# A two-layer streaming encoder in float32: the first chunk's norm from token-major x, the u columns of the next group turned one product earlier, and B's weight pieces moved off the v steps

## The chip, the cores and the metric

The kernel runs on one core of a Trainium2 chip. The metric is the device time of one execution in microseconds (us), the median of several runs. Five engines work side by side, each through its own list of instructions in a fixed order: PE (TensorE, matrix products), DVE (VectorE), ACT (ScalarE), POOL (GpSimd) and SP (SyncE, which here only issues DMA transfers). An engine stops at an instruction whose inputs are not there, and everything behind it on that engine stops too.

## The reference

The stream `x` has 2048 tokens of 1024 channels. Layer A mixes by causal pooling, layer B by stick-breaking attention; after each comes a gated embedding add.

```python
def pool_mixer(h, w_in, w_group, scale, w_out):
    u, z = jnp.split(h @ w_in, 2, axis=-1)
    ...   # means over the last 2, 4, 8, 16 frames in four channel groups, minus the frame itself
    mixed = jnp.einsum('bsgc,gcd->bsgd', pooled, w_group).reshape(B, S, D_MODEL) * scale
    return (mixed * jax.nn.silu(z)) @ w_out
...
h = rms_norm(x, a_norm[i])
x = x + pool_mixer(h, a_w_in[i], a_w_group[i], a_scale[i], a_w_out[i])
kv_in = rms_norm(x, kv_norm)
k_all, v_all = jnp.split(kv_in @ w_kv, 2, axis=-1)
k_sh = rms_norm(split_heads(k_all), k_norm)
q, z = jnp.split(rms_norm(x, b_norm[j]) @ b_w_in[j], 2, axis=-1)
q = rms_norm(split_heads(q), b_q_norm[j])
o = stick_breaking_attention(q, k_sh, v_sh)
x = x + (o * jax.nn.silu(z)) @ b_w_out[j]
x = x + (p[i] @ ple_w[i]) * jax.nn.sigmoid(x @ ple_gate_w[i])
```

## The kernel before

**Numbers in two halves.** Every float32 operand is split into a rounded high half and the remainder. ACT writes the high half, DVE or POOL the low one, and PE makes three products of each pair (high by high, high by low, low by high; lines 164 to 166). A pair of a weight is a *unit*, tile `wpair`, from two pools of six; its raw form is `wraw`.

**Chunks and steps.** The dense part runs over four chunks of 512 tokens. A chunk has 22 steps (`STEPS`): z and u columns of the four groups in turn (steps 0 to 7: z3, u3, z2, u2, z1, u1, z0, u0), the output projection (8 to 11), the gate (12 to 15), then two steps each for q, k and v (16 to 21). Ahead of a step the loop at line 806 converts the next step's weights and fetches those of the step after it. The attention follows the fourth chunk.

**Folding in the first chunk.** The linear map of a group is folded into the u columns, once, in chunk 0. `load_fold` (line 396) asks for the columns (`uraw`, two tiles of 128x1024) and for the group's map. `fold` (line 410) works in eight pieces: four times `across` (line 417) turns a part of the columns into a pair `wt`, four times `mapped` (line 424) makes 12 matmuls (line 431) and converts the result into a unit (lines 438 and 439), which the group's u step multiplies by and which is stored to DRAM for the later chunks. Group 3 is folded inside step z3 (`first_beside`); group g-1 inside the u step of group g (`second_beside`, line 455): columns in the first four of the product's eight parts, `mapped` behind parts 5 to 8.

**The norm of the first chunk.** The squares of all eight `x` tiles (channels by tokens) are taken on ACT (line 326) and summed on DVE (328); `summed` (299) turns the sum with four small matmuls, POOL makes the inverse root, and `bcast` (240) lays it over the partitions. z3 and u3 are scaled by it (485, 503), then come the running sums (509), the gate and the halves `mp` of the result.

**Order.** The engines' lists are made by a scheduler that may move instructions; `tc.keep_in_program_order` pins one to its place in the program. SP issues its transfers in program order (`queue`, line 87). The pinned ones here are those of step z3 and of group 3's fold.

**B's pieces.** 56 pieces of layer B's weights (`kept`) are fetched, split and stored beside the dense steps; line 835 decides at which.

Of the kernel before, what the change touches and what calls it, by code (L numbers as in the profile page):

```python
# [14 lines left out]
P = 128  # L15
# [19 lines left out]
def trunk_kernel(ctx, tc, x, xt, pt0, wut, cols, heads, zin, grp, aout, agate, aple,  # L35
# [63 lines left out]
    class Weights:  # L99
# [29 lines left out]
        def convert(self, half=0):  # L129
            kk, n, gain, kept, c0 = self.kk, self.n, self.gain, self.kept, self.c0  # L130
            self.reread()
            for k0 in self.part(half):
# [6 lines left out]
                if gain is None:  # L139
                    self.stay(A.copy(out=pr[:, 0], in_=raw))  # L140
                    state["w"] += 1
                    (G if state["w"] % 3 else V).tensor_tensor(out=pr[:, 1], in0=raw, in1=f(pr[:, 0]), op=ALU.subtract)  # L142
# [74 lines left out]
    with ExitStack() as st:  # L217
# [59 lines left out]
        def load_tokens(s, q):  # L277

            xn = f(pair("xn")).rearrange("q e n -> q (e n)")
            t0 = s * W5 + q * P  # L280
            queue(out=xn, in_=x[0, t0 : t0 + P, :])
            chunk[s].setdefault("xn", []).append(xn)

        def prep(s):
# [14 lines left out]
            def summed():  # L299
                acc = chunk[0].pop("acc0")  # L300
                ps = turned()
                for j in range(4):
                    T.matmul(ps[:, 0, j : j + 1], acc[:, j * P : (j + 1) * P], ones, start=True, stop=True)
                A.copy(out=parts, in_=ps[:, 0, 0:4])
                norm()

            if not s:
                chunk[0]["summed"] = summed
# [13 lines left out]
            if s:  # L322
                return
            for o in range(KT):
                sq = tmp("sqx")
                stay(A.activation(out=sq, in_=xs[o], func=AF.Square))
                if o:
                    V.tensor_tensor(out=acc, in0=acc, in1=sq, op=ALU.add)
                else:
                    acc = sq  # L330
                if o % 4 == 3:
                    yield
            chunk[0]["acc0"] = acc

        wz0 = {"raw": [], "pair": []}

        def load_first(g):
# [3 lines left out]
            for q in range(4):  # L341
# [4 lines left out]
                if not q:  # L346
                    load_gains()
# [24 lines left out]
        def first_beside():  # L372
# [6 lines left out]
            def behind():  # L379
                for kt in range(KT):  # L380
                    next(lead, None)
                    if kt == 7:
                        for _ in lead:
                            pass
                        chunk[0]["fold"][2] = load_fold(2)
# [3 lines left out]
                    if kt > 2:  # L389
                        next(folded, None)  # L390
                    yield
# [4 lines left out]
        def load_fold(g):  # L396
# [3 lines left out]
            if g < 3:  # L400
                maps[g] = Weights(grp[g], 2, 0, 256)
                maps[g].fetch()
            for ct in range(2):
# [3 lines left out]
                raws.append(raw)  # L407
            return raws, wg

        def fold(g, raws, wg):  # L410
# [4 lines left out]
            stay = tc.keep_in_program_order if g == 3 else lambda ins: ins  # L415
# [29 lines left out]
            for i in range(4):  # L445
                across(i)
                if i == 2 and g < 3:
                    maps[g].convert()
# [5 lines left out]

        def second_beside(g):
# [764 lines left out]
```

## Time and profile before

| | us |
|---|---|
| median of three runs | 2733.45 |
| lowest, highest | 2730.84, 2734.16 |
| the profiled execution, its own time | 2732.34 |
| its span, first to last instruction | 2730.6 |

The page gives busy times of 2688.7 us for PE, 1983.8 for DVE, 1366.5 for ACT and 879.0 for POOL. Times in the trace count from the first instruction. In a row of the timeline stand start, length, engine, line, operation, tiles and, in brackets, the idle time just before it with what ended it. Matmuls are pipelined, so the distance of two starts, and not the length shown, is what one costs.

### The profile page before, as it was taken

How to read it: one execution, taken by the hardware profiler on the slowest of the kernel's cores; microseconds unless marked ns; L12 is line 12 of the kernel's file. 1: busy time of each engine (PE TensorE's matmuls, PEld its weight loads, DVE VectorE, ACT ScalarE, POOL GpSimd, SP SyncE). 2: the span in 40 equal slices, each digit the busy share in tenths (PEclk: the TensorE clock that was granted, in tenths of full speed). 3: DMA queues.
4: the chain of work that ended last, by engine and by line, in shares of the span. 5: the costliest groups of instructions: out<-in, count | busy, mean ns of one | idle time of the engine just before them, and what ended most of it. 6: DMA issues, size and time to landing. Idle time of an engine off the chain costs nothing.

```text
span 2730.6 us, 38583 instructions
## 1 busy us (share of the span) xinstructions
PE 2688.7 (98%) x13360; PEld 2228.9 (82%) x13360; DVE 1983.8 (73%) x2572; ACT 1366.5 (50%) x2672; POOL 879.0 (32%) x695
## 2 busy tenths in 40 slices
PE   8999999999999999999999999999999999999999
PEld 7888888888888888888878888887887778888877
DVE  6777635665366643755399999999999998997632
ACT  5445532455234541445356556666666665655430
POOL 2574337643485435753121111110110111112220
PEclk9999999999999999999999999999999999999999
DMA  7646696466955679444688675555555566668965
GB/s 276 219 158 234 247 321 218 167 238 247 319 190 192 231 259 317 143 148 158 215 249 276 190 226 169 167 163 170 173 156 166 162 198 208 192 200 258 268 227 170
DMA packets 275968, 579.46 MB, mean 212 GB/s; under 512 B 33047, under 2 KB 66839, under 8 KB 275773
## 3 DMA queue, kind: packets, MB, share of 16 engines
q1 hardware_dynamic: 270034, 569.31, 63.5%
q10 hardware_dynamic: 5738, 7.68, 1.0%
q8 instruction: 106, 1.74, 0.3%
q14 instruction: 90, 0.73, 0.1%
HBM read 436.30 MB, written 132.19 MB: 208 GB/s over the span
## 4 chain that ended last, share of the span: by engine, by line
PE 81%; DVE 10%; issue 3%; DMA 2%; POOL 2%; ACT 1%; SPq 1%; ACTq 0%; DVEq 0%; POOLq 0%
PE psd L613 18%; PE psd L164 8%; PE psd L165 8%; PE psd L166 8%; PE psa L939 7%; PE psd L983 5%; PE psd L985 5%; PE psd L987 5%; DVE pp L926 4%; PE pso L952 3%; PE psl L915 3%; PE pso L951 3%; PE psl L914 3%; DVE at L943 2%; PE pst L718 1%
## 5 line engine op out<-in xcount | busy, mean ns | idle before, releaser
L942 ACT CAST at<-psa 128x512 fp32r<-128x512 f32 (+3 forms) x640 | 334.8, 523 | 481.6 <-PE psa L939 463.8
L613 PE MATMUL psd<-wpair,x 128*128 128x512 f32 x2304 | 537.5, 392 | 0.9 <-DVE x L254 0.9
L926 DVE TENSOR_TENSOR_SCAN pp<-kap,pp,zeros 128x512 f32<-128x512 f32 x384 | 514.7, 1340 | 3.0 <-ACT kap L918 2.5
L613 PEld LDWEIGHTS psd<-wpair,x 128*128 128x128 f32 x2304 | 429.8, 188 | 88.9 <-DVE x L254 1.7
L943 DVE TENSOR_TENSOR at<-psa,at 128x512 fp32r<-128x512 f32 (+3 forms) x640 | 381.1, 596 | 82.9 <-ACT at L942 79.5
L939 PE MATMUL psa<-ident,pp 128*128 128x128 f32 x2176 | 346.9, 275 | 21.5 <-DVE at L943 20.2
L918 ACT ACTIVATE kap<-psl 128x512 f32<-128x512 f32 (+3 forms) x640 | 345.2, 539 | 14.0 <-PE psl L915 11.2
L939 PEld LDWEIGHTS psa<-ident,pp 128*128 128x128 f32 x2176 | 262.9, 140 | 98.1 <-DVE at L943 45.8
L914 PE MATMUL psl<-kk,qa 128*128 128x512 f32 (+3 forms) x640 | 281.9, 440 | 0.0
L952 PE MATMUL pso<-at,vv 128*128 128x512 f32 (+3 forms) x640 | 234.7, 367 | 0.8 <-DVE at L943 0.8
L915 PE MATMUL psl<-kk,qb 128*128 128x512 f32 (+3 forms) x640 | 232.7, 364 | 0.0
L951 PE MATMUL pso<-at,vv 128*128 128x512 f32 (+3 forms) x640 | 231.9, 362 | 0.0
L923 DVE TENSOR_TENSOR_SCAN pp<-kap,ahead 128x128 f32<-128x128 f32 (+3 forms) x256 | 223.9, 875 | 5.3 <-ACT kap L918 3.9
L164 PE MATMUL psd<-xp,wpair 128*128 128x512 f32 x512 | 201.6, 394 | 3.6 <-DVE wpair L439 3.5
L165 PE MATMUL psd<-xp,wpair 128*128 128x512 f32 x512 | 200.6, 392 | 2.1 <-DVE xp L314 2.1
L166 PE MATMUL psd<-xp,wpair 128*128 128x512 f32 x512 | 200.4, 392 | 0.0
L147 DVE SCALAR_TENSOR_TENSOR wpair<-wraw,gains,wpair 128x512 fp32r<-128x512 f32 x192 | 156.2, 854 | 59.1 <-ACT wpair L146 59.1
L1021 POOL TENSOR_TENSOR zr<-zr,sgz 128x512 f32<-128x512 f32 x32 | 59.1, 1845 | 371.0 <-ACT sgz L1020 342.8
L142 POOL TENSOR_TENSOR wpair<-wraw,wpair 128x512 fp32r<-128x512 f32 x99 | 145.5, 1480 | 101.0 <-ACT wpair L140 98.0
L146 ACT ACTIVATE wpair<-wraw,gains 128x512 fp32r<-128x512 f32 x192 | 132.6, 718 | 74.0 <-DMA wraw<-in_bq_dram 36.6
L140 ACT CAST wpair<-wraw 128x512 fp32r<-128x512 f32 x148 | 90.2, 619 | 127.4 <-PE psd L166 100.3
L952 PEld LDWEIGHTS pso<-at,vv 128*128 128x128 f32 x640 | 120.2, 188 | 27.9 <-DVE at L943 1.5
(199 smaller groups left out, 5350.9 us busy)
## 6 DMA issues: line engine op xcount, KB each, us to landing
kk<-kd SPq DMA_DIRECT2D x320, 128.0 KB
vv<-vd SPq DMA_DIRECT2D x160, 256.0 KB
wraw<-in_kv_dram SPq DMA_DIRECT2D x128, 256.0 KB
wpair<-wzd SPq DMA_DIRECT2D x64, 512.0 KB
wpair<-wod SPq DMA_DIRECT2D x64, 512.0 KB
wpair<-wgd SPq DMA_DIRECT2D x64, 512.0 KB
wpair<-wu SPq DMA_DIRECT2D x48, 512.0 KB
wpair<-wi SPq DMA_DIRECT2D x36, 512.0 KB
```

Of the source, the lines that this page charges most:

```text
L164: T.matmul(ps, wst(units, kt, 0, c0), acts[kt][:, 0], start=(begin and kt == order[0]), stop=False)
L165: T.matmul(ps, wst(units, kt, 0, c0), acts[kt][:, 1], start=False, stop=False)
L166: T.matmul(ps, wst(units, kt, 1, c0), acts[kt][:, 0], start=False, stop=(end and kt == order[-1]))
L613: T.matmul(pss2[i], ck["x2"][kt][:, xh, tk], wst(ws, kt, wh, 0, W5), start=(kt == 0 and xh == 0 and wh == 0), stop=(kt == KT - 1 and wh == 1))
L914: T.matmul(ps[:, :w], qa[:, qs], kk[:, :w], start=True, stop=False)
L915: T.matmul(ps[:, :w], qb[:, qs], kk[:, :w], start=False, stop=True)
L918: A.activation(out=kp[:, r0:], in_=ps[:, :w], func=AF.Sigmoid, scale=-1.0)
L926: V.tensor_tensor_scan(out=pp[:, ::-1], data0=kp[:, ::-1], data1=zeros.to_broadcast([P, W5]), initial=st["carry"][j], op0=ALU.mult, op1=AL ...
L939: T.transpose(pt[:, j * P : (j + 1) * P], pp[:, r0 + kt * P : r0 + (kt + 1) * P], ident)
L942: A.copy(out=at[:, 0, cs], in_=pt[:, cs])
L943: V.tensor_tensor(out=at[:, 1, cs], in0=pt[:, cs], in1=f(at[:, 0, cs]), op=ALU.subtract)
L952: T.matmul(po[:, cs], vv[:, kt, :], at[:, 1, cs], start=False, stop=(st["last"] and kt == 3))
```

## The change

1. **Norm from tokens.** In chunk 0 the squares are taken as in the other chunks: `x` is loaded once more, tokens by channels (four tiles `xn` of 512 KB, from the four buffers `t4`), and ACT squares and sums a tile in one instruction, in the first four parts of step u3. The eight squares, seven adds and the four small matmuls go.
2. **Columns a product ahead.** Group 2's columns and map are asked for right behind group 3's; group 1's at the start of step u3, group 0's at that of step u2. `turning` does the four `across` and the map's conversion inside the z step before; the u step only makes `mapped`. For group 2 the four `across` stay in step u3, but all of a fold's instructions on ACT and DVE are pinned.
3. **Head norms.** The product of the two head gains (`gqk`, DVE) moves from the first instructions of chunk 0 to step u3.
4. **B's pieces.** None is fetched at v steps; steps 12 to 15 (12 to 17 in chunk 0) fetch two each.

```diff
@@ class Weights, convert
-                    (G if state["w"] % 3 else V).tensor_tensor(out=pr[:, 1], in0=raw, in1=f(pr[:, 0]), op=ALU.subtract)
+                    self.stay((G if state["w"] % 3 else V).tensor_tensor(
+                        out=pr[:, 1], in0=raw, in1=f(pr[:, 0]), op=ALU.subtract))
@@ load_tokens
-            xn = f(pair("xn")).rearrange("q e n -> q (e n)")
+            xn = pair("xn") if s else t2.tile([P, 2, W5], F32R, tag="t4", name="xn", bufs=4)
+            xn = f(xn).rearrange("q e n -> q (e n)")
@@ prep
-            def summed():
...
+            def all_squares():
+                for q in range(4):
+                    squares(q)
+                    if q == 3:
+                        norm()
+                    yield
...
-            for o in range(KT):
-                sq = tmp("sqx")
-                stay(A.activation(out=sq, in_=xs[o], func=AF.Square))
...
@@ first_beside
-                    if kt == 7:
-                        for _ in lead:
-                            pass
-                        chunk[0]["fold"][2] = load_fold(2)
...
+                    if kt == 7:
+                        maps[2].convert()
@@ load_fold, fold
-            if g < 3:
-                maps[g] = Weights(grp[g], 2, 0, 256)
-                maps[g].fetch()
...
+            if g < 3:
+                maps[g] = Weights(grp[g], 2, 0, 256, stay=tc.keep_in_program_order)
+                maps[g].fetch()
...
-            stay = tc.keep_in_program_order if g == 3 else lambda ins: ins
+            stay = tc.keep_in_program_order
@@ new, and second_beside
+        def turning(g):
+
+            chunk[0]["fold"][g] = folded = fold(g, *chunk[0]["fold"][g])
+            for kt in range(KT):
+                if kt == 2:
+                    maps[g].convert()
+                if 2 < kt < 7:
+                    next(folded)
+                yield
+
         def second_beside(g):
-            folded = fold(g, *chunk[0]["fold"].pop(g))
+            folded = chunk[0]["fold"].pop(g)
+            if g == 2:
+                folded = fold(g, *folded)
             for kt in range(KT):
-                next(folded, None)
-                if kt == 4 and "summed" in chunk[0]:
-                    chunk[0].pop("summed")()
+                if g == 2 or kt > 3:
+                    next(folded, None)
+                if g == 2:
+                    next(chunk[0]["squares"], None)
                 yield
@@ run_z
+            elif not s and g:
+                beside = turning(g - 1)
@@ the loop over the steps
+            if i in (1, 3):
+                chunk[0]["fold"][1 - i // 2] = load_fold(1 - i // 2)
...
             elif not i:
                 feed(2, "fetch")
+                for q in range(4):
+                    load_tokens(0, q)
+            elif i == 1:
+                join_gains(wz0["gs"])
+                feed(3, "fetch")
...
-            if not s and step in (2, 4):
-                chunk[0]["fold"][2 - step // 2] = load_fold(2 - step // 2)
-            if step >= (8 if s else 10) and (s + 1 < NSUB or step < 16):
+            if (8 if s else 10) <= step < (20 if s + 1 < NSUB else 16):
                 kept.pop(0)()
-                if s + 1 < NSUB and step in ((8, 12) if s else (10, 12, 14, 16)):
+                if s + 1 < NSUB and 12 <= step < (16 if s else 18):
                     kept.pop(0)()
```

The list of PE keeps its order except for the four small matmuls. Three other lists show what moves. A row names the source line, the operation and the tiles with their buffer numbers; the changed file has ten lines more, so that 438 and 439 of before are 425 and 426, 420 and 421 are 407 and 408, and 146 is 148 there.

SP, behind the map of group 3 (`in_grp`), before: `in_zin` are z2's weights, `in_wut` the columns, `wz0` the stores of z3's units.

```order
L89 DMA wraw_391<-in_grp_dram 128x512
L89 DMA wraw_408<-in_zin_dram 128x512
L89 DMA wraw_410<-in_zin_dram 128x512
L89 DMA wraw_412<-in_zin_dram 128x512
L89 DMA wraw_414<-in_zin_dram 128x512
L89 DMA wraw_549<-in_grp_dram 128x512
L89 DMA uraw_551<-in_wut_dram 128x1024
L89 DMA uraw_553<-in_wut_dram 128x1024
L89 DMA wz0_0_631<-wpair_417 128x1024
L89 DMA wz0_1_633<-wpair_436 128x1024
```

And in the change:

```order
L90 DMA uraw_392<-in_wut_dram 128x1024
L90 DMA uraw_394<-in_wut_dram 128x1024
L90 DMA wraw_396<-in_grp_dram 128x512
L90 DMA wraw_413<-in_zin_dram 128x512
L90 DMA wraw_415<-in_zin_dram 128x512
L90 DMA wraw_417<-in_zin_dram 128x512
L90 DMA wraw_419<-in_zin_dram 128x512
L90 DMA xn_421<-in_x_dram 128x1024
L90 DMA xn_423<-in_x_dram 128x1024
L90 DMA xn_425<-in_x_dram 128x1024
L90 DMA xn_427<-in_x_dram 128x1024
L90 DMA wz0_0_618<-wpair_430 128x1024
```

Group 2's columns stand ahead of z2's weights now, and the four token tiles stand between these and the stores.

ACT, behind the last column pairs of group 3, before, with the semaphores waited for in brackets (`DMAHW` is a transfer): `psd` to `wpair` is the high half of group 3's units, `uraw_551` and `uraw_553` are group 2's columns.

```order
L438 ACTIVATE wpair_568<-psd_555,g_a_100 128x256 [waits PE_49]
L420 CAST wt_671<-uraw_551 128x512 [waits DMAHW7_49]
L438 ACTIVATE wpair_568<-psd_555,g_a_100 128x256 [waits DVE_49]
L438 ACTIVATE wpair_587<-psd_574,g_a_100 128x256 [waits PE_49]
L420 CAST wt_680<-uraw_553 128x512 [waits DMAHW0_49]
L420 CAST wt_689<-uraw_551 128x512 [waits Activation_49]
L438 ACTIVATE wpair_587<-psd_574,g_a_100 128x256 [waits DVE_49]
L438 ACTIVATE wpair_606<-psd_593,g_a_100 128x256 [waits PE_49]
```

And in the change, from the last unit of group 3 on: `wpair_638` and `wpair_644` are the last two units of z2, `xn` the token tiles.

```order
L148 ACTIVATE wpair_638<-wraw_417,g_a_100 128x256 [waits DMAHW7_49,DMAHW5_49,Activation_49]
L425 ACTIVATE wpair_612<-psd_599,g_a_100 128x256 [waits DVE_49]
L148 ACTIVATE wpair_638<-wraw_417,g_a_100 128x256
L148 ACTIVATE wpair_644<-wraw_419,g_a_100 128x256 [waits DMAHW6_49,DMAHW0_49,Activation_49]
L148 ACTIVATE wpair_644<-wraw_419,g_a_100 128x256
L407 CAST wt_665<-uraw_392 128x512 [waits DMAHW2_49,Activation_49]
L295 ACTIVATE xn_421,parts_429<-xn_421 128x1024 [waits DMAHW1_49]
L407 CAST wt_675<-uraw_394 128x512 [waits DMAHW3_49,Activation_49]
L295 ACTIVATE xn_423,parts_429<-xn_423 128x1024 [waits DMAHW2_49]
```

The conversions of group 2's columns stood among those of group 3's units and now stand behind them, and behind z2's; the third and the fourth unit of z2 each wait for two transfers, their raw weights and the store that frees their buffer.

DVE, behind the pooling of group 3 (`po`, `zr`), before: `uraw_887` and `uraw_889` are group 1's columns, `psd_891` and `psd_892` the z2 product.

```order
L519 SCALAR_TENSOR_TENSOR po_870<-po_870,gains_101,zr_834 128x512
L485 TENSOR_TENSOR zr_949<-psd_891,rbx_827 128x512
L147 SCALAR_TENSOR_TENSOR wpair_977<-wraw_883,g_a_100,wpair_977 128x256
L142 TENSOR_TENSOR wpair_1012<-wraw_885,wpair_1012 128x512
L485 TENSOR_TENSOR zr_954<-psd_892,rbx_827 128x512
L421 TENSOR_TENSOR wt_991<-uraw_887,wt_991 128x512
L421 TENSOR_TENSOR wt_1000<-uraw_889,wt_1000 128x512
L421 TENSOR_TENSOR wt_1009<-uraw_887,wt_1009 128x512
L421 TENSOR_TENSOR wt_1025<-uraw_889,wt_1025 128x512
```

And in the change, where group 1's columns are `uraw_650` and `uraw_652`:

```order
L520 SCALAR_TENSOR_TENSOR po_859<-po_859,gains_101,zr_823 128x512
L143 TENSOR_TENSOR wpair_894<-wraw_654,wpair_894 128x512
L408 TENSOR_TENSOR wt_907<-uraw_650,wt_907 128x512
L408 TENSOR_TENSOR wt_916<-uraw_652,wt_916 128x512
L408 TENSOR_TENSOR wt_925<-uraw_650,wt_925 128x512
L408 TENSOR_TENSOR wt_934<-uraw_652,wt_934 128x512
L486 TENSOR_TENSOR zr_947<-psd_874,rbx_816 128x512
L149 SCALAR_TENSOR_TENSOR wpair_963<-wraw_868,g_a_100,wpair_963 128x256
L486 TENSOR_TENSOR zr_952<-psd_875,rbx_816 128x512
```

Group 1's column pairs stood behind the two reads of the finished z2 product and now stand ahead of them, right behind the pooling of group 3.

More of the change, by code (lines that the diff above doesn't have):

```diff
@@ L1 @@
+import itertools
 from contextlib import ExitStack
@@ L297, in norm @@
                 chunk[s]["r"] = r
-            def summed():
[L300 to L305, printed above, removed]
+            def all_squares():
[4 more added lines that the diff above has]
+                    yield
             if not s:
-                chunk[0]["summed"] = summed
+                chunk[0]["squares"] = all_squares()
             for o in range(KT):
@@ L446, in fold @@
                 across(i)
-                if i == 2 and g < 3:
-                    maps[g].convert()
+                if i == 3 and g < 3:
                     wg.extend(maps[g].units)
@@ L792, in trunk_kernel @@
         maps[3].fetch()
+        chunk[0]["fold"][2] = load_fold(2)
         state["first"] = False
```

13 lines of the change are left out of this document (3 added, 10 removed).

## The prediction

> **What bounds the kernel now.** I began with the page's list of engines and the waits of PE by the engine waited for (us in all, times, longest).
>
> ```profile
> PE 2688.7 (98%) x13360; PEld 2228.9 (82%) x13360; DVE 1983.8 (73%) x2572; ACT 1366.5 (50%) x2672; POOL 879.0 (32%) x695
> ```
>
> ```profile
> PE psa L939 <- DVE at L943: 20.2, 33, 2.2
> PE psd L164 <- DVE wpair L439: 3.5, 1, 3.5
> PE psd L165 <- DVE xp L314: 2.1, 3, 1.3
> ...
> PE psd L431 <- DVE wt L421: 2.0, 2, 1.3
> ...
> PE psd L431 <- ACT wt L420: 1.0, 1, 1.0
> ...
> PE psd L613 <- DVE x L254: 0.9, 2, 0.7
> ```
>
> PE works for 98% of the span. Half of what it waits is in the attention (L939), which the change doesn't touch; of the rest nearly all is in step z3, at the start of step u3 (L164) and at group 1's fold (L431). The windows say where (us, busy time of PE, PEld, DVE, ACT, POOL, granted clock, DMA share, GB/s):
>
> ```profile
> 31.00:68.30 37.30, 37.30 (x186) 31.69 (x186) 27.22 (x49) 17.85 (x41) 13.23 (x14) 0.96 0.76 289
> 68.30:75.00 6.70, 3.62 (x14) 2.79 (x14) 6.70 (x8) 3.72 (x7) 5.37 (x3) 0.75 0.87 296
> 75.00:105.00 30.00, 30.00 (x149) 25.72 (x149) 21.52 (x36) 12.36 (x26) 12.34 (x13) 0.94 0.58 219
> 105.00:1320.00 1215.00, 1213.42 (x5509) 1004.91 (x5509) 705.52 (x878) 531.80 (x930) 639.13 (x527) 1.00 0.64 222
> ```
>
> Between 105 and 1320 us PE lacks 1.6 us. So whatever the change gives lies before 80 us, and each us of PE's list there is a us of the end, since no engine behind has to be waited for. The PE timeline of the two places:
>
> ```profile
> 21.52 5.90 PE L431 MATMUL psd<-wpair,wt 128*128 128x256 f32 x48
> 30.97 0.80 PE L164 MATMUL psd<-xp,wpair 128*128 128x512 f32 x1 [3.54 <-DVE wpair L439]
> ...
> 34.12 0.40 PE L165 MATMUL psd<-xp,wpair 128*128 128x512 f32 x1
> ...
> 39.36 1.59 PE L431 MATMUL psd<-wpair,wt 128*128 128x256 f32 x12
> 40.80 0.95 PE L303 MATMUL pst<-ones,sqx 128*128 128x1 f32 x8
> 41.60 0.48 PE L164 MATMUL psd<-xp,wpair 128*128 128x512 f32 x1
> ...
> 48.67 0.60 PE L244 MATMUL pst<-ident,rx 128*128 128x128 f32 x4
> ...
> 68.05 0.39 PE L166 MATMUL psd<-xp,wpair 128*128 128x512 f32 x1
> 69.47 0.81 PE L431 MATMUL psd<-wpair,wt 128*128 128x256 f32 x2 [1.03 <-ACT wt L420]
> 71.58 0.97 PE L431 MATMUL psd<-wpair,wt 128*128 128x256 f32 x3 [1.30 <-DVE wt L421]
> 73.26 1.86 PE L431 MATMUL psd<-wpair,wt 128*128 128x256 f32 x7 [0.71 <-DVE wt L421]
> 74.92 0.63 PE L164 MATMUL psd<-xp,wpair 128*128 128x512 f32 x1
> ...
> 77.48 2.04 PE L431 MATMUL psd<-wpair,wt 128*128 128x256 f32 x12
> 79.36 0.40 PE L164 MATMUL psd<-xp,wpair 128*128 128x512 f32 x1
> ```
>
> A 512-wide product costs 0.228 us (23 of them from 34.12 to 39.36), twelve of L431 cost 1.44 (39.36 to 40.80). Behind each wait PE is slower for a while: the seven products from 30.97 to 34.12 take 3.15 instead of 1.59, 1.56 too long; the granted clock of that window is 0.96, of the next place 0.75 and 0.94.
>
> **What the places cost.** Place one: 3.54 of waiting, 1.56 of slow clock, and 0.80 for L303 (40.80 to 41.60), which the change removes: **5.90**. Place two: from 68.28, where the last product ends (68.05 + 0.23), to 74.92 stand 6.64 for work of 1.44, so 5.20; the six products up to 77.48 take 2.56 instead of 1.37, 1.19; the next twelve of L431 1.88 instead of 1.44, 0.44: **6.83**. Together 12.7.
>
> **Place one after the change.** Why PE waited there is on ACT and DVE:
>
> ```profile
> 16.90 0.62 ACT L140 CAST wpair<-wraw 128x512 fp32r<-128x512 f32 x1 [0.34 <-DMA wraw<-in_grp_dram]
> ...
> 29.18 0.62 ACT L420 CAST wt<-uraw 128x512 fp32r<-128x512 f32 x1 [4.64 <-DMA uraw<-in_wut_dram]
> ```
>
> The first unit's second half stood behind group 2's columns, whose transfer landed at 29.18. In the change those conversions are pinned behind group 3's, so u3 starts where L431 ends, at 27.4, and the wait and its slow clock go. ACT's eight squares and DVE's seven adds stood behind it too; nobody waited for them but this unit.
>
> What is late next: behind 30 products of u3 (27.4 + 6.84 = 34.2) PE wants group 2's column pairs, the second of them three matmuls (0.36) later, at 34.6. On ACT these stand behind z2's last two units, which wait for the stores of z3's first two. Those stores stand behind much on SP: from the landing of group 3's map, 16.9, there pass two columns (a 128x1024 tile is 0.52 MB), a map (0.26), four raw weights (1.05), four token tiles (2.10) and two stores (1.05), 5.5 MB in all. The rates that this stretch shows:
>
> ```profile
> 16.50:19.00 2.50, 2.22 (x8) 1.05 (x6) 2.02 (x3) 2.16 (x6) 1.29 (x1) 1.00 0.00 0
> 21.00:27.00 6.00, 6.00 (x49) 5.87 (x49) 5.48 (x10) 3.54 (x8) 0.00 (x0) 1.00 0.92 276
> 27.00:30.00 3.00, 0.43 (x4) 0.22 (x2) 0.40 (x2) 0.82 (x2) 0.00 (x0) 1.00 1.01 412
> ```
>
> ```profile
> 18.92 1.92 SPq L89 DMA_DIRECT2D wraw<-in_zin_dram  x4
> ```
>
> The zero is a hole: SP issued z2's weights only at 18.92, and that hole closes, because they no longer need a buffer held that long. At 412 GB/s the second store lands at 30.3, at 276 at 36.8. I take 276 for the narrow rows (1.31 MB, 4.7 us) and 412 for the wide ones (4.19 MB, 10.2), 31.8. Behind it come two L146, L420, a square, L420 and DVE's L421, by these rows (last numbers: total, mean ns):
>
> ```profile
> L421 DVE TENSOR_TENSOR wt<-uraw,wt 128x512 fp32r<-128x512 f32 x16 | 15.5, 996 | 5.4 <-ACT wt L420 5.4
> ...
> L147 DVE SCALAR_TENSOR_TENSOR wpair<-wraw,g_a,wpair 128x256 fp32r<-128x256 f32 x24 | 13.8, 601 | 0.0
> ...
> L292 ACT ACTIVATE xn<-xn 128x1024 f32<-128x1024 f32 x12 | 12.6, 1051 | 0.0
> ...
> L146 ACT ACTIVATE wpair<-wraw,g_a 128x256 fp32r<-128x256 f32 x24 | 10.6, 503 | 0.0
> ...
> L420 ACT CAST wt<-uraw 128x512 fp32r<-128x512 f32 x16 | 9.4, 615 | 8.0 <-DMA uraw<-in_wut_dram 8.0
> ```
>
> That is 1.0 + 0.6 + 1.05 + 0.6 + 0.7 (an undisturbed L421), 4.0: ready at 35.8, a new wait of **1.2**. Ends: ready at 34.3, no wait; ready at 40.8, 6.2, with 1.6 of slow clock 7.8. I charge no clock for 1.2. On that the Trainium skill ("TensorE: Matmul & The Clock Gate", What's actually happening) says that the clock halves after an idle window of about 3.4 us. The trace doesn't agree: the clock was low at 74.92 after waits of 1.03, 1.30 and 0.71 between matmuls. By the page the new wait is 1.2, by that row it can be 2.8. A rule that speaks against the change is in "DMA: Bandwidth & Descriptors" (Queues, rings and completion order): an engine takes descriptors in ring order, so the stores can't pass the tokens. The sum has that order already, from SP's list.
>
> The squares end behind the fourth column, some 4 us later, well before `bcast` is due (9 us behind 34.6); POOL's root needs about 1.2.
>
> **Place two after the change.** These rows of DVE and POOL show what PE waited for:
>
> ```profile
> 67.51 0.74 DVE L519 SCALAR_TENSOR_TENSOR po<-po,gains,zr 128x512 f32<-128x512 f32 x1
> ...
> 70.37 5.13 DVE L421 TENSOR_TENSOR wt<-uraw,wt 128x512 fp32r<-128x512 f32 x4
> ```
>
> ```profile
> 70.94 3.41 POOL L487 TENSOR_TENSOR zr<-zr,sg 128x512 f32<-128x512 f32 x2
> ```
>
> Counted from `bcast` (48.67), the pooling of group 3 ends on DVE after 19.6 (68.25), and the pairs came from 21.7 on, at 1.28 each beside POOL. PE wanted them at 19.6 (68.28). In the change `bcast` stays the origin, with PE's list as it was, so PE wants them at 19.6 again, the second at 20.0. Ahead of the pairs go five L147 (3.0) and two reads of z2; one L439 (0.5) and the map's remainder (0.7) come: they start at 19.6 - 3.0 + 0.5 + 0.7 = 17.8. The second is ready at 19.2 (0.7 each) to 20.4 (1.28 each): a wait of 0 to **0.4**; I take 0.4. Ends: 0 and 2.5, if POOL's part and not DVE's own list sets the pace.
>
> **The rest.** The head norms' product held DVE's first subtraction for PE's first wait of 1.3; PE then waits again for `x` tiles whose ACT casts stand behind the columns' landing, so it is absorbed: 0, ends 0 and -1.3. B's pieces lie under a PE that is busy; 0, ends -0.9 (the L613 wait at the start of q) and +3. The 2 MB of tokens cost nothing but the stores' delay.
>
> **Sum.** 12.7 - 1.2 - 0.4 = 11.1; the profiled execution took 2732.34, so 2721.2. The median of the runs is 1.1 above that execution; I give half of it on, **2721.8**.
>
> **Rivals.**
> - *The stores set the pace* (R1): at 276 GB/s, place one loses 7.8 and the gain is 4.5: 2728.4 with the same half. For it: the rate of 276 lasted six us. Against: the hole in front of it. Chance 0.18.
> - *The pairs stay late* (R2): group 1's pairs come at 21.7 as before, second ready at 24.3, a wait of 4.3 and 1.6 of clock. Gain 12.7 - 1.2 - 5.9 = 5.6: 2727.3. For it: POOL's chain is not shortened. Chance 0.13.
> - *Slower* (R3): in steps 13 and 15 one more piece each brings 0.26 MB in and 0.52 out ahead of q's weights. At 349 GB/s that is 2.2 us each:
>
> ```profile
> 230.00:240.00 10.00, 10.00 (x45) 8.27 (x45) 6.64 (x8) 3.27 (x6) 2.27 (x2) 1.00 1.01 349
> ```
>
> If q's first unit is late by both, 4.5 us and 1.6 of clock in three chunks are 18: 2739.9. It turns the sign from 3.7 a chunk on. For it: the queue is full there. Against: PE waited 0.9 there in all chunks together. Chance 0.08.
> - My forecast has 0.55; 0.06 is left for small mixtures.
>
> **Chances and range.** About 0.2% (5.5 us) is what a measurement can tell from no change. The forecast, R2 and half of R1 lie below 2728: faster 0.76; the rest of R1 and mixtures: same 0.16; slower 0.08. The best case, all 12.7, the q wait and the first 1.3, is 2717.4, not all at once, so 2718.5. At the top R1 with R2's end of 2.5 is 2731; I end at 2730.
>
> **What would show it.** Right: no wait at the first L164 of step u3; a short wait of the first L431 of group 2's fold, ended by ACT or DVE `wt`; none above 1 us at group 1's fold; clock 1.00 from 60 us on; L303 gone. Wrong: a wait of 4 us or more at either fold (R1, R2), or a new wait at L613 (R3).

## The result, and the profile after

| | before | changed |
|---|---|---|
| median of 6 runs (us) | 2733.53 | 2716.44 |
| lowest to highest | 2730.84 to 2737.03 | 2715.06 to 2720.76 |
| profiled execution, its span | 2730.6 | 2713.6 |

The ratio is 0.9940, 95% interval 0.9927 to 0.9953: 17 us less. I had forecast 2721.8 in a range of 2718.5 to 2730.0; the time lies 2.1 us below the range. The direction was right and the gain half as large again as forecast (17.1 against 11.7).

The page's list of engines and the waits of PE of the changed kernel (us in all, times, longest):

```profile
PE 2681.3 (99%) x13352; PEld 2224.8 (82%) x13352; DVE 1967.6 (73%) x2565; ACT 1365.9 (50%) x2671; POOL 874.5 (32%) x695
```

```profile
PE psa L949 <- DVE at L953: 20.2, 35, 2.2
PE psd L167 <- DVE xp L316: 1.5, 2, 0.9
...
PE psd L418 <- ACT wt L407: 0.3, 1, 0.3
PE psd L418 <- DVE wt L408: 0.2, 1, 0.2
```

The 3.5 at the start of step u3 is gone. So are the 3.0 at group 1's fold (2.0 and 1.0); 0.5 came at group 2's. The q products' 0.9 has left the list as well, which I had not counted on. The windows of the two places (PE first, granted clock third from the end):

```profile
31.00:50.00 19.00, 18.48 (x105) 15.96 (x104) 8.61 (x15) 13.59 (x26) 5.69 (x7) 1.00 0.99 398
...
68.30:80.00 11.70, 11.70 (x61) 9.71 (x60) 9.48 (x20) 6.95 (x16) 4.51 (x7) 1.00 0.97 350
```

The PE timeline of the changed kernel at the rows that answer to those of before (L418 is L431 of before, L166 is L164, L246 is L244):

```profile
20.23 5.91 PE L418 MATMUL psd<-wpair,wt 128*128 128x256 f32 x48
25.97 0.40 PE L166 MATMUL psd<-xp,wpair 128*128 128x512 f32 x1
...
32.83 0.51 PE L418 MATMUL psd<-wpair,wt 128*128 128x256 f32 x3
33.64 0.50 PE L418 MATMUL psd<-wpair,wt 128*128 128x256 f32 x2 [0.30 <-ACT wt L407]
34.36 1.10 PE L418 MATMUL psd<-wpair,wt 128*128 128x256 f32 x7 [0.22 <-DVE wt L408]
35.30 0.40 PE L166 MATMUL psd<-xp,wpair 128*128 128x512 f32 x1
...
42.30 0.60 PE L246 MATMUL pst<-ident,rx 128*128 128x128 f32 x4
...
61.91 1.65 PE L418 MATMUL psd<-wpair,wt 128*128 128x256 f32 x12
...
64.79 1.60 PE L418 MATMUL psd<-wpair,wt 128*128 128x256 f32 x12
```

PE's list is the same in both kernels but for the eight records of L303 and a few products that change places, so the two traces can be laid over each other product by product. The lead of the changed kernel over the first execution of before (start before, start after, us):

| PE at | before | after | lead | gained since the row above |
|---|---|---|---|---|
| group 3's fold | 21.52 | 20.23 | 1.3 | 1.3 |
| first product of u3 | 30.97 | 25.97 | 5.0 | 3.7 |
| group 2's fold | 39.36 | 32.83 | 6.5 | 1.5 |
| broadcast of the norm | 48.67 | 42.30 | 6.4 | -0.2 |
| second part of group 1's fold | 77.48 | 64.79 | 12.7 | 6.3 |
| q of chunk 0, last wait | 243.59 | 229.22 | 14.4 | 1.7 |
| q of chunk 1, its small products | 570.14 | 554.99 | 15.2 | 0.8 |
| a product in the attention | 1400.22 | 1383.53 | 16.7 | 1.5 |
| end of the last product | 2725.08 | 2708.18 | 16.9 | 0.2 |

So the two places of the forecast gave about what they should (11.4 of the 16.9, the step from the first row's 1.3 to 12.7), and 5.5 us came from elsewhere: 1.3 before the first fold, 4.2 behind the second part of group 1's (0.2 up to 86 us, 2.4 at the q steps of chunks 0 and 1, 1.5 in the attention). The experiments had to say which of these belong to the change, and to what in it.

### The profile page after: what moved, and what is told of

It reads as the page before. It is cut to its first block, busy times and chain, and to the rows that moved or that the text cites. A ratio compares the mean times of both kernels' runs of the same rounds, so it can differ in the third digit from the quotient of the medians.

```text
span 2713.6 us, 38599 instructions
## 1 busy us (share of the span) xinstructions
PE 2681.3 (99%) x13352; PEld 2224.8 (82%) x13352; DVE 1967.6 (73%) x2565; ACT 1365.9 (50%) x2671; POOL 874.5 (32%) x695
## 4 chain that ended last, share of the span: by engine, by line
PE 85%; DVE 10%; issue 2%; DMA 2%; ACT 1%; POOL 0%; SPq 0%; ACTq 0%; DVEq 0%; POOLq 0%
PE psd L614 19%; PE psd L166 9%; PE psd L167 9%; PE psd L168 9%; PE psa L949 7%; PE psd L993 5%; PE psd L995 5%; PE psd L997 5%; DVE pp L936 5%; PE pso L962 3%; PE psl L925 3%; PE pso L961 3%; PE psl L924 3%; DVE at L953 3%; PE pst L719 1%
## 5 line engine op out<-in xcount | busy, mean ns | idle before, releaser
L166 PE MATMUL psd<-xp,wpair 128*128 128x512 f32 x512 | 199.9, 391 | 0.0
L143 POOL TENSOR_TENSOR wpair<-wraw,wpair 128x512 fp32r<-128x512 f32 x99 | 144.4, 1468 | 81.2 <-ACT wpair L141 76.6
```

The source lines that it names most:

```text
L166: T.matmul(ps, wst(units, kt, 0, c0), acts[kt][:, 0], start=(begin and kt == order[0]), stop=False)
```

## The experiments

The kernel before is timed beside every run, on the same chip, five rounds each. Its medians were 2731.95, 2731.93 and 2734.24 in the three groups of runs. "More" or "less" than the changed kernel is measured from its 2716.46 of the first group. That group ran on another chip than the other two, and before's medians differ by 2.3 between the groups, so across groups a difference of 1 or 2 us proves nothing by itself.

**The same two kernels again.** No edit.

> The kernel before, profiled a second time, to tell what belongs to the code from what one execution happened to do. The lead of the changed kernel over the kernel before, product by product of PE, grew by 1.3 us before the fold of group 3, by 0.8 at the q step of chunk 1 (570 us) and by 1.5 at a wait for layer B's weights in the attention (1400 us); none of the three was in the forecast. If they belong to the code: here again the fold of group 3 starts at 21.5 us (within 0.3), the wait of 1.3 for the stored weights in the attention is there, and the time is 2733.5 within 2. Rival, they are the chance of one execution: the fold starts by 20.5 us here or the wait in the attention is gone.

> The changed kernel, profiled a second time, timed in five more rounds. If the three terms belong to the code: the fold of group 3 starts at 20.2 us (within 0.3), no wait for stored weights in the attention, 2716.4 within 2. Rival: the fold starts at 21 us or later, or waits of about 1 us appear at other places.

Before: 2732.43, ratio 1.0001 (0.9992 to 1.0010). Changed: 2716.46, ratio 0.9943 (0.9930 to 0.9955). The PE timelines of the second executions, of before and of the changed kernel:

```profile
21.20 5.90 PE L431 MATMUL psd<-wpair,wt 128*128 128x256 f32 x48
```

```profile
21.40 5.92 PE L418 MATMUL psd<-wpair,wt 128*128 128x256 f32 x48
```

Group 3's fold starts at 21.52 and 21.20 in the two executions of before and at 20.23 and 21.40 in those of the changed kernel. The 1.3 of the first row is chance: it follows the landing of group 3's columns, which moves by over 1 us between executions of one kernel. The second execution of the changed kernel reaches the fold of group 2 later by 1.2, and PE loses only 0.35 there (33.98 to 35.77, for 1.44 of work), so 0.7 of that 1.2 is made up again.

Laid over each other, the second executions give the changed kernel 5.4 from group 3's fold to the end of group 2's, 5.8 at group 1's fold, 0.8 at the output projection of chunk 0 (140 us), and 3.6 at the q steps of chunks 0 and 1. The wait in the attention is smaller here (the lead grows by 0.7 there and not 1.5). It doesn't go with the table of the pieces: the run with the channel norm has 0.8 of it with the new table, and the run with the old table, next, has none. Whether it belongs to the rest of the change stays open.

**The old table of B's pieces** in the changed kernel.

```diff
-            if (8 if s else 10) <= step < (20 if s + 1 < NSUB else 16):
+            if step >= (8 if s else 10) and (s + 1 < NSUB or step < 16):
                 kept.pop(0)()
-                if s + 1 < NSUB and 12 <= step < (16 if s else 18):
+                if s + 1 < NSUB and step in ((8, 12) if s else (10, 12, 14, 16)):
                     kept.pop(0)()
```

> The changed kernel with the old table for layer B's pieces. If the new table is what took the waits at the start of the q steps away: the waits of 0.9 us at the q products and of 0.5 at the sums of chunk 1 come back, PE is the same as in the changed kernel up to 220 us and 2 to 2.5 us later behind chunk 1: 2718.5 to 2719. Rival (the waits went because the steps before reached the q step in another state, or by chance): no wait comes back, 2716.4 within 0.5. My forecast's own reading was 0, with 0.9 as the end of the range.

2720.63, ratio 0.9962 (0.9950 to 0.9975): 4.2 us more than the changed kernel. None of its five runs was below 2719.7, none of the changed kernel's five beside it above 2716.7. The waits of the q steps are back (PE's waits, the old table):

```profile
PE psd L614 <- DVE x L256: 0.9, 2, 0.7
...
PE pst L625 <- POOL acc L599: 0.6, 1, 0.6
...
PE psd L614 <- ACT x L255: 0.4, 1, 0.4
```

Laid over the second execution of the changed kernel, it falls behind by 0.8 at 140 us, 0.5 at the q step of chunk 0, 2.7 at that of chunk 1, 0.5 at that of chunk 2. The theory held, with more than it said, and my forecast's 0 fell. Nothing in it told why.

**The channel norm of before** in the changed kernel: no token tiles; squares, sums and the small products of before.

```diff
-                for q in range(4):
-                    load_tokens(0, q)
...
+            for o in range(KT):
+                sq = tmp("sqx")
+                stay(A.activation(out=sq, in_=xs[o], func=AF.Square))
+                if o:
+                    V.tensor_tensor(out=acc, in0=acc, in1=sq, op=ALU.add)
...
+                        for _ in lead:
+                            pass
                         maps[2].convert()
...
+                if kt == 4 and "summed" in chunk[0]:
+                    chunk[0].pop("summed")()
```

> The changed kernel with the squares and sums of the channel tiles and the four small products of before, and without the token tiles. My forecast charged the tokens with the delay of the stores (1.2 us of new wait) and credited the small products with 0.8: by it this is 2716 to 2717, with no wait at the fold of group 2 and 0.8 of small products. Rival: the token norm matters because it frees the eight x tiles' buffers and ACT at the end of step z3: here the weights of z2 are asked for at 17 us or later (11.5 in the changed kernel), the squares stand ahead of the conversions of group 3's units, PE waits 1 to 2 us at the start of step u3, and the time is 2718.5 to 2721.

2719.00, ratio 0.9951 (0.9939 to 0.9964): 2.5 us more. SP's and PE's timelines of this kernel:

```profile
10.04 1.69 SPq L90 DMA_DIRECT2D uraw<-in_wut_dram  x2
18.58 0.33 SPq L90 DMA_DIRECT2D wraw<-in_grp_dram  x1
19.00 1.97 SPq L90 DMA_DIRECT2D wraw<-in_zin_dram  x4
```

```profile
27.96 0.50 PE L166 MATMUL psd<-xp,wpair 128*128 128x512 f32 x1 [0.87 <-DVE wpair L442]
...
35.22 0.95 PE L306 MATMUL pst<-ones,sqx 128*128 128x1 f32 x8
```

The rival was right in its mechanism and at the low end of its size: z2's weights are asked for at 19.0 (11.5 in the changed kernel), PE waits 0.87 at the start of u3, where it waits for nothing in the changed kernel, and the small products are back. The wait is made on DVE, where the sums of the squares stand ahead of the second half of group 3's first unit (L442, which starts when they end):

```profile
23.41 3.07 DVE L331 TENSOR_TENSOR sqx<-sqx 128x512 f32<-128x512 f32 x4
```

Laid over the second execution of the changed kernel, 1.7 of the loss comes here, up to group 2's fold, and 0.9 at the open wait in the attention.

**Two pins with the old table.**

```diff
-                V.tensor_tensor(out=sgs[k], in0=pls[k], in1=sgs[k], op=ALU.mult)
-                V.tensor_tensor(out=ts[k], in0=sgs[k], in1=ts[k], op=ALU.add)
+                tc.keep_in_program_order(V.tensor_tensor(out=sgs[k], in0=pls[k], in1=sgs[k], op=ALU.mult))
+                tc.keep_in_program_order(V.tensor_tensor(out=ts[k], in0=sgs[k], in1=ts[k], op=ALU.add))
...
+                        if n == W5 and not half:
+                            tc.keep_in_program_order(ins)
```

> The old table of the pieces, as in the run before that cost 4.2 us, but with the sums of the gate steps and the first-half conversions of the wide weights pinned on DVE, so that two conversions of q's weights instead of five stand ahead of the third gate step's sums. Theory: the old table costs time through DVE's list alone: a conversion of q's weights that waits for its transfer (2.6 us in chunk 0, 3.5 in chunk 1) holds the gate's sums behind it, these hold a store on SP, and q's other weights, queued behind that store, come late. By it the waits at the q products go although the table is the old one: 2716.5 to 2717.5. Rival: the old table's transfers themselves are what delays q's weights: 2720 to 2721, with waits of about 1 us at the q products as in that run.

2722.35, ratio 0.9962 (0.9950 to 0.9975): above the rival's range too, and a miss. But the edit didn't do what it was meant to. DVE's list in it has the second half of q's weights ahead of the third gate step's sums and the first half behind: the pin ties an instruction to its neighbour in the program, and that neighbour had itself been moved ahead. The question was asked again below.

**Turning in the u step again**, for groups 1 and 0.

```diff
-            elif not s and g:
-                beside = turning(g - 1)
...
-            if g == 2:
-                folded = fold(g, *folded)
+            folded = fold(g, *folded)
...
-                if g == 2 or kt > 3:
-                    next(folded, None)
+                next(folded, None)
```

> The changed kernel, but the columns of groups 1 and 0 are turned in the u step before their use, unpinned, as before the change; they are asked for as early as in the changed kernel. Theory of the forecast: group 1's column pairs again stand behind the pooling of group 3 on DVE and come at 21.7 us behind the broadcast of the norm while PE wants them at 19.6: waits of about 3 us at group 1's fold and a low clock behind them, 6.8 in all: 2723.3 (2722 to 2724). Rival: asking early, and the shorter list without squares, is what made group 1's pairs early: below 2718.5.

The pins of these two groups' folds and map conversions are taken out as well, and the map is again converted behind the third column pair. 2726.79, ratio 0.9977 (0.9967 to 0.9986): 10.3 us more. PE and DVE at group 1's fold:

```profile
64.50 0.39 PE L418 MATMUL psd<-wpair,wt 128*128 128x256 f32 x1 [1.52 <-ACT wt L407]
70.33 2.71 PE L418 MATMUL psd<-wpair,wt 128*128 128x256 f32 x11 [5.44 <-DVE wpair L143]
```

```profile
63.14 4.73 DVE L149 SCALAR_TENSOR_TENSOR wpair<-wraw,g_a,wpair 128x256 fp32r<-128x256 f32 x5
67.79 1.88 DVE L408 TENSOR_TENSOR wt<-uraw,wt 128x512 fp32r<-128x512 f32 x3
69.60 0.68 DVE L143 TENSOR_TENSOR wpair<-wraw,wpair 128x512 fp32r<-128x512 f32 x1
```

The rival, that asking early is what made the pairs early, is dead: the columns were asked for as early as in the changed kernel. The place in the list decides. It cost more than the 6.8 of the forecast, because here the map's remainder (L143) stood behind the pairs as well: PE waits 7.0 in the two rows, and the granted clock is 0.50 from 65.31 to 75.55.

**Group 2's columns asked for late**, pins kept.

```diff
-        chunk[0]["fold"][2] = load_fold(2)
         state["first"] = False
...
                     if kt == 7:
-                        maps[2].convert()
+                        chunk[0]["fold"][2] = load_fold(2)
```

> The changed kernel, but group 2's columns and map are asked for at the end of step z3, behind z2's weights and the token tiles, as before the change; all pins stay. Theory: the wait at the start of step u3 went because the conversions of group 2's columns are pinned behind those of group 3's units, not because the columns come earlier. By it PE does not wait there; the columns land near 26 us, before ACT gets to them, and the time is that of the changed kernel, 2716 to 2717.5. Rival: the early asking is needed: a wait of 1 us or more at the start of step u3 or at group 2's fold, 2718.5 to 2721.

2717.47, ratio 0.9940 (0.9927 to 0.9954), within 1.0 of the changed kernel. The fold of group 3 takes from 22.05 to 27.79, and step u3 starts there without a wait:

```profile
22.05 5.91 PE L418 MATMUL psd<-wpair,wt 128*128 128x256 f32 x48
27.79 0.40 PE L166 MATMUL psd<-xp,wpair 128*128 128x512 f32 x1
```

So the first place didn't go because group 2's columns are asked for early. That the pins behind group 3's units took it away is argued from ACT's list: no run takes these pins out alone, and the token norm stays in this one. The pins alone would not have done it all, since with the channel norm 0.87 of the wait is back.

**Squares later, head gains pinned.**

```diff
-                if g == 2:
+                if g == 2 and kt > 1:
                     next(chunk[0]["squares"], None)
...
-            V.scalar_tensor_tensor(out=gqk, in0=gs[:, 1:2], scalar=HD ** -0.5, in1=gs[:, 0:1],
-                                   op0=ALU.mult, op1=ALU.mult)
+            tc.keep_in_program_order(V.scalar_tensor_tensor(
+                out=gqk, in0=gs[:, 1:2], scalar=HD ** -0.5, in1=gs[:, 0:1], op0=ALU.mult, op1=ALU.mult))
```

> The changed kernel with two edits that may gain: the token squares start two parts later in step u3, behind three of the four column conversions, and the product of the head gains is pinned on DVE so that it really leaves the first place of DVE's list (in the changed kernel the scheduler put it back there, and DVE waits for its transfer until 7.6 us). Theory one: the wait at group 2's fold is made by the squares between the column conversions and goes (0.9 us), and the first wait of PE gets shorter but is absorbed, since the later x tiles stand on ACT behind group 3's columns, which land at 13.7 to 15: 2715 to 2716. Rival one: the earlier start is kept too: 2714 to 2715. Rival two: the squares, now later, make the root late for the broadcast: 2717 or more.

2715.55, ratio 0.9936 (0.9923 to 0.9948); 0.9 less than the changed kernel, which the intervals don't separate. The fold of group 2 has no wait, but the broadcast gets one for the root, as the second rival said (its time, 2717 or more, didn't come):

```profile
42.34 0.65 PE L246 MATMUL pst<-ident,rx 128*128 128x128 f32 x4 [0.50 <-POOL rx L81]
```

**An edge in DVE's list, with the old table.** One edge more and no other edit. SP's transfers and PE's products keep the order of the old table. On ACT and POOL the scheduler moved a few instructions along with it: at the gate steps the split of a piece (`kpair`) now stands behind the instructions that take the gate's result, and no longer ahead of them.

```diff
+                state["sum"] = V.tensor_tensor(out=ts[k], in0=sgs[k], in1=ts[k], op=ALU.add)
...
+                        if gain is g_b and "sum" in state and (half if c0 == 0 else not half):
+                            tc.add_manual_dep(
+                                ins.ins, state["sum"].ins.name,
+                                mybir.DependencyInfo(mybir.DependencyClass.NoSync, mybir.DependencyReason.DATA),
+                                reason="behind the sums")
```

> The old table of the pieces again, with all transfers as in it, and one edge added to DVE's list: the conversions of q's second half, and those of the next q step's first half, may not be placed ahead of the gate sums that are written before them in the program. (The run with pins had missed this: its pins tied the conversions to a neighbour that was itself moved ahead, and put the second half ahead of the first.) Theory: with one conversion less ahead of the third gate step's sums, DVE does not wait there (2.6 us in chunk 0, 3.5 in chunk 1 with the old table), the stores on SP and q's weights behind them come early, and the waits at the q products go: 2716.5 to 2717.8. Rival: the table's transfers or ACT's list, not DVE's, set it: 2719.5 to 2721, with the waits of about 1 us at the q products.

2716.55 (2716.34 to 2717.28), ratio 0.9941 (0.9927 to 0.9955): the changed kernel's time and ratio with the old table. The theory held. Of the rival, the transfers are dead; ACT's list moved along with DVE's and isn't tested apart, but the conversion's wait of 3.45 below, ahead of the sums, is on DVE. Laid over the second execution of the changed kernel, this one loses nothing at the q steps any more, where the old table lost 3.7. It still loses 0.8 at 140 us, so that part has another cause, which stays open. Here are the rows of DVE at the gate steps of chunk 1 with the old table, first without the edge:

```profile
532.87 0.74 DVE L149 SCALAR_TENSOR_TENSOR wpair<-wraw,gains,wpair 128x512 fp32r<-128x512 f32 x1
537.06 0.75 DVE L149 SCALAR_TENSOR_TENSOR wpair<-wraw,gains,wpair 128x512 fp32r<-128x512 f32 x1 [3.45 <-ACT wpair L148]
537.73 1.28 DVE L583 TENSOR_TENSOR sg<-psd,sg 128x512 f32<-128x512 f32 x2
...
552.70 0.75 DVE L149 SCALAR_TENSOR_TENSOR wpair<-wraw,gains,wpair 128x512 fp32r<-128x512 f32 x1 [3.94 <-ACT wpair L148]
553.37 1.28 DVE L583 TENSOR_TENSOR sg<-psd,sg 128x512 f32<-128x512 f32 x2
```

and with it:

```profile
531.41 1.37 DVE L588 TENSOR_TENSOR sg<-psd,sg 128x512 f32<-128x512 f32 x2
532.70 1.28 DVE L589 TENSOR_TENSOR tx<-sg,tx 128x512 f32<-128x512 f32 x2
535.08 0.75 DVE L149 SCALAR_TENSOR_TENSOR wpair<-wraw,gains,wpair 128x512 fp32r<-128x512 f32 x1 [1.10 <-ACT wpair L148]
...
545.06 1.32 DVE L588 TENSOR_TENSOR sg<-psd,sg 128x512 f32<-128x512 f32 x2
```

SP between the two, without the edge and with it (x2d is the store of a gate step's result, the eight are q's other weights):

```profile
539.64 0.33 SPq L90 DMA_DIRECT2D x2d<-tx  x1
...
546.30 5.39 SPq L90 DMA_DIRECT2D wraw<-in_bq_dram  x8
```

```profile
533.40 0.33 SPq L90 DMA_DIRECT2D x2d<-tx  x1
...
540.98 5.06 SPq L90 DMA_DIRECT2D wraw<-in_bq_dram  x8
```

This is a loop through four lists. A conversion of q's weights that waits for its transfer (3.45) stands on DVE ahead of the gate's sums, which are ready. Behind the sums stands their store on SP, and behind that store the request for q's next weights, 546.30 against 540.98. They land late, and their conversions again stand ahead of the next sums (3.94). Those sums make the last `x` tiles of the q product, and PE waits.

**The new table alone**, in the kernel before.

> The kernel before with the new table of the pieces and nothing else. Theory: the table is worth the same 4.2 us here as undoing it cost in the changed kernel: 2727 to 2728.5, and its times scatter less than those of before (2728 to 2737). Rival: it helps only with the rest of the change: 2731 to 2733.

2727.55, ratio 0.9977 (0.9968 to 0.9987): 6.7 us less than before. The table acts without the rest of the change, and its 4.2 in the changed kernel lies in the interval (3.6 to 8.7). The times spread over 6.2 us, before's beside them over 8.8. PE's waits at the q products are gone from the list here too.

**Two tries at more.** The squares one part later (`if g == 2 and kt:`), and this together with the pin of the head gains and the edge on DVE.

> The changed kernel with the token squares one part later in step u3: two of the four column conversions stand ahead of the first square, the last square stands between group 2's units. Theory: the first two units of the fold need only the first two column pairs, so the wait at group 2's fold goes (0.9 us) and, unlike in the run with two parts, the root is ready for the broadcast: 2715.3 to 2716. Rival: the wait moves to the third unit of the fold or the broadcast: 2716.2 to 2717.

> The changed kernel with three edits: the squares as in the run beside this one, the head gains' product pinned behind z2's conversions, and the edge of the first run of this call that keeps q's conversions behind the gate sums on DVE. Theory: the first gives 0.9, the second next to nothing (absorbed by the landing of group 3's columns, or 0.5), the third nothing or a little, as the new table already has a good list: 2714.8 to 2715.8. Rival: the edge delays q's first-half conversions and a wait of about 1 us appears at a q product: 2717 or more.

2716.78 (0.9941, 0.9928 to 0.9954) and 2717.19 (0.9942, 0.9929 to 0.9955): neither gains. Both times are in their rivals' ranges, but the waits that the rivals named, at the fold, the broadcast or a q product, didn't come. The wait at group 2's fold goes in both, but the fold also begins later, at 33.9 and 34.9, since step z3 started late in these executions. What 0.9 us there is worth can't be told apart from the landing of the first transfers.

## Why the prediction was wrong

**The step that failed** is in "The rest": "B's pieces lie under a PE that is busy; 0, ends -0.9 (the L613 wait at the start of q) and +3." Measured, it is 4.2 us off the time, undone in the changed kernel, and 6.7 alone. With 4.2 in the sum the forecast is 2717.6, and the whole gain is accounted for within its interval. That the first comparison also had 4.2 behind group 1's fold is chance: there 1.5 of it was the wait in the attention, and 2.4 the q steps. I had looked for what the pieces move (bytes ahead of q's weights, the rival R3) and not for what they change in the lists. The lists show it. DVE ahead of and behind the third gate step's sums of chunk 0, before and after the change (instruction, tiles):

```
before  L147 wpair_2374   L147 wpair_2461   L582 sg2_2343   L582 sg2_2344
after   L149 wpair_2357   L583 sg2_2326   L583 sg2_2327   ...   L149 wpair_2446
```

One conversion changed sides. `wpair_2461` belongs to the second half of q's weights, whose transfer is still on its way when the sums are ready. DVE in the execution of before that I read:

```profile
221.12 0.75 DVE L147 SCALAR_TENSOR_TENSOR wpair<-wraw,gains,wpair 128x512 fp32r<-128x512 f32 x1 [3.28 <-ACT wpair L146]
```

The waits of the trace made it look small: 0.9 at q in all chunks. With that, "whatever the change gives lies before 80 us" fell as well. The three waits of that execution at the q steps (0.23 and 0.70, and 0.48 at the small products) put PE back by 2.4 against the changed kernel, about 0.3 more each than the idle time shown. And they were one execution's. Before's runs span 2728.5 to 2738.4 over all groups, the changed kernel's 2715.1 to 2720.8, those of the old table with the edge 2716.3 to 2717.3 (five runs). In the second execution of before the q steps of chunks 0 and 1 wait 2.4 us (1.0, 0.8 and 0.6) and lose 3.6 against the changed kernel.

**R3**, a slowdown by pieces ahead of q's weights: the sign was the other. Two pieces in steps 13 and 15 delayed nothing that was waited for.

**Place one** (5.90): right. From group 3's fold to group 2's the lead grew by 3.7 and 1.5, and L303 was 0.8: 6.0 (5.8 in the second executions). The run with the channel norm bears out the prediction's reading that the squares and sums held the same unit.

**Place two** (6.83, less 0.4 for a new wait): right, with 6.3 up to the second part of the fold and 0.4 more in it (5.8 in all in the second executions); no wait was left. The pairs came just in time. They began 18.8 behind the broadcast, 1.0 later than forecast, but each took 0.62, where the sum had 0.7 to 1.28; that the two misses cancelled is luck:

```profile
61.13 2.48 DVE L408 TENSOR_TENSOR wt<-uraw,wt 128x512 fp32r<-128x512 f32 x4
```

R2 is out.

**The new wait at group 2's fold** (1.2): near in size, wrong in its cause. The fold took 2.47 (32.83 to 35.30) for 1.44 of work, so 1.0; in the second execution, where PE comes later, it is 0.35, so the size was luck too. ACT's rows:

```profile
30.60 0.91 ACT L148 ACTIVATE wpair<-wraw,g_a 128x256 fp32r<-128x256 f32 x2 [0.16 <-DMA wz<-wpair]
31.42 0.60 ACT L407 CAST wt<-uraw 128x512 fp32r<-128x512 f32 x1
31.93 1.06 ACT L295 ACTIVATE xn<-xn 128x1024 f32<-128x1024 f32 x1
32.89 0.18 ACT L295 ACTIVATION_READ_ACCUMULATOR xn<-xn 128x1 f32 x1
32.98 0.60 ACT L407 CAST wt<-uraw 128x512 fp32r<-128x512 f32 x1
```

The store held ACT for 0.16; the square between the two conversions, which the sum had too, made the second late. Both stores had landed by 30.6, which is the sum at 412 GB/s throughout (30.3), not the 31.8 that I took: from 12 to 31 us the transfers run at 392 to 422 GB/s. R1 is out.

**Head norms**: 0 was right, but not as argued. The product did not move: the scheduler put it back into the first place of DVE's list. In the run that pins it, a product of PE that starts at 8.42 here, behind 0.94 of waiting, starts at 7.22, and by 16.4 us the two are level; there the lead is absorbed, as the forecast said.

```profile
7.59 0.16 DVE L742 SCALAR_TENSOR_TENSOR gqk<-gs 128x1 f32<-128x1 f32 x1 [5.61 <-DMA gs<-in_heads_dram]
```

**The token norm** I credited with 0.8 for L303 and charged with the stores' delay. Taking it back cost 2.5, of which the trace shows 1.7 in its place: the small products, and the squares and sums ahead of group 3's units. That z2's weights are asked for late, too, made no wait that shows. The 0.9 in the attention isn't explained by it.

Open: the 0.7 to 1.5 us at a wait for stored weights in the attention, which differs between executions of one kernel, and the 0.8 at the output projection of chunk 0 with the old table.

## What to carry to other kernels

A change that only moves hidden work can still move an engine's list by one place, and that place can be worth more than the work. Where a scheduler makes the lists, compare them around every wait of the critical engine, and look there for an instruction that waits for a transfer and stands ahead of ready work: behind it stores, requests and the next transfers come late in a loop. And where a kernel's times scatter by 10 us, as before's did, profile it twice before a small wait is priced: here the waits at the q steps were 1.4 us in one execution and 2.4 in the next.

## What the runs showed of the hardware

The low clock comes in stretches of 3.41 us or whole multiples, but for the one that the end of an execution cuts off (3.41 at 30.7, 6.83 at 71.7 in the first execution of before), on a grid that goes through the whole execution: from 30.7 to 71.7 there are 12 of them. The windows of before on this grid:

```profile
27.31:30.72 3.41, 0.12 (x2) 0.00 (x0) 0.89 (x2) 1.54 (x4) 0.00 (x0) 0.99 1.02 419
30.72:34.13 3.41, 3.16 (x8) 2.52 (x9) 3.41 (x9) 3.41 (x10) 0.00 (x0) 0.50 1.03 422
```

```profile
68.27:71.68 3.41, 1.03 (x4) 0.48 (x3) 3.41 (x6) 3.40 (x7) 2.70 (x2) 0.99 0.75 270
71.68:75.10 3.42, 2.71 (x11) 2.42 (x12) 3.42 (x3) 0.34 (x1) 2.67 (x2) 0.50 0.99 325
```

A window in which PE was busy for 0.12 or 1.03 of 3.41 us is followed by one at half the clock. Over the executions of this case windows with less than 1.5 us of work were followed by the low clock, and with 2.1 or more at the full clock they were not; between these both occur. The Trainium skill ("TensorE: Matmul & The Clock Gate", What's actually happening) has a free-running window of this length and the low clock after an idle one. The runs agree with the grid; that a window need not be empty for it is what they add, and with it the row of the prediction that I read as speaking against the page (waits of 1.03, 1.30 and 0.71, low clock) is explained: together the first two of these waits left 1.03 us of work in one window. Whether a wait of 2 us costs a slow window thus depends on where it falls on the grid. So in the attention: near 2160 us the second execution of the changed kernel has a window with 1.21 us of work and 3.41 us of low clock behind it, while the first has 1.75 in its emptiest window there and keeps the full clock; that parts the two by 0.6 us.
